# Seven block products for the output projection of layer 0, with operand sums made in DRAM

## The chip, the cores and the metric

The kernel runs on one core of a Trainium2 chip. The metric is the device time of one execution in microseconds, the median of three runs: 1484.73 (1484.15 to 1485.28). A profiled execution, with its trace, gives the rows that are quoted below.

## The reference

Two diffusion blocks work on 768 tokens (512 image tokens and 256 context tokens) of width 1024. Layer 0 mixes tokens by a long convolution (hyena) and by grouped attention with 8 heads, multiplies both with a gate, and projects the 2048 columns together back to 1024; layer 1 is an mLSTM over the same tokens. What the change touches is the projection at the end of layer 0 and what stands around it:

```python
def combine(hy, att, g_hy, g_att):
    return jnp.concatenate([hy * jax.nn.silu(g_hy), att * jax.nn.silu(g_att)], axis=-1) @ w_out

sh_l, sc_l, ga_l = adaln(c, w_mod[layer], b_mod[layer])      # gate rows: the third part, ga
...
x_lat = x_lat + ga_l[:, None] * rms_norm(y_lat, g_post[layer])
```

## The kernel before

All products keep float32 accuracy by parts: each operand is split into a high and a low half (`split`: ScalarE casts the high half, VectorE subtracts to get the low one), and `mm3` issues three matmuls for one product. Weights come through `load_w`: a slice of 1024 x 256 is loaded in two halves of 512 KB on SP's queue into `wr` (three buffers) and split into `wh` and `wl`.

The program consists of regions: `hy` (convolution), `att` (attention), `out0` (the output projection of layer 0 and the next layer's normalised tokens), `l1a` and `l1b` (layer 1) and `out1` (its output projection). `record` collects the instructions of a region, and `play` issues them in the order of a table of numbers, ORDERS, written out for each region; all engines take their instructions in that order. `SLOTS` says which buffer a tile gets. So all instructions have the line of the helper, L998, in the profile, and are told apart by their tiles: `pj` and `pm` are PSUM tiles of products and small products, `hTh` and `hTl` the transposed tokens (8 k-tiles x 768 tokens) as the stationary operand, `yoh` and `yol` the same for the attention's part of layer 0's mix, `yacc` the accumulated output.

The 2048 columns of the mix are sixteen rows of 768 tokens in a DRAM tensor, `y_scratch` (in the code `y0`): 0 to 7 from the convolution, stored in `hy`, and 8 to 15 from the attention's heads, each stored when its head is done in `att`. The attention loop runs over n = 0 to 23 (head n // 3, a third of the queries n % 3): it transposes probabilities (`turned`), computes the next scores, does what `plan[n]` lists, and multiplies by the values. Through GpSimd's queue the convolution's rows are loaded at n = 18 and 19 and split into `hTh`, `hTl`. `plan` 20 to 23 and `rest` hold `stage_a`: a first half of the projection, 256 output columns at a time, for six token tiles (12 tiles of 24 matmuls, 256 wide).

In `out0`, `out_stages` does the other two column groups of the first half in the same way, then the attention's half of the mix with matmuls 512 wide, added to `yacc` by VectorE; when a token tile's second half of the columns is complete, it is squared, weighed by the gate row `gg`, normalised, added to the input, stored, normalised again (`epi0`) and transposed into `hTh`, `hTl` by `h_tile`, from which layer 1 starts. `gate_rows` makes a gate row out of two 1 MB slices of `w_mod` by 32 small matmuls (32x256, `pm` from `cond`), and spreads it over the partitions by one more. Layer 0's gate rows stand in `out0`, layer 1's at the end of `l1b` (`heads`, the last head).

Layer 1's output projection and its gate products `o` and `z` are already computed as seven block products, with the sums of weight blocks made in DRAM by copies on SP and accumulating transfers on GpSimd's queue (`o_sums`, `w_sums`).

Of the kernel before, what the change touches and what calls it, by code (L numbers as in the profile page):

```python
# [2893 lines left out]
```

## Time and profile before

The profile's page holds busy times of the engines, the DMA queues, the chain of work that ended last, and groups of instructions. PE is TensorE's matmul, PEld its weight loads, DVE VectorE, ACT ScalarE, POOL GpSimd, and SP the engine that issues most transfers.

| | |
|---|---|
| median of the runs | 1484.73 us |
| the profiled execution | 1486.4 us, span 1484.6 us |
| out0 begins, l1a begins (PE) | 743.4, 878.8 us |
| last head stored in att (SP) | 732.0 us |
| layer 1's gate rows (PE, end of l1b) | 1378 to 1400 us |
| DMA, whole span | 230.93 MB, mean 156 GB/s |
| transfers of 512 KB for layer 1's sums | o_sums 28 on POOL, 28 on SP; w_sums 16 on POOL, 16 on SP |

PE is busy over the whole span, so the question for every part is whether PE waits there, and for whom. Windows of 20 us answer that: they give each engine's busy time in the stretch, with the clock granted to TensorE and the share of the DMA engines.

### The profile page before, as it was taken

To read this page: it belongs to the slowest core of one execution; us is meant where nothing else is said; L and a number is where in the kernel's file an instruction comes from. 1 tells how busy PE (TensorE), PEld (TensorE's weight loads), DVE (VectorE), ACT (ScalarE), POOL (GpSimd) and SP (SyncE) were. 2 spreads that over 40 slices of the span, in tenths; PEclk is the share of its full clock that TensorE was granted. 3 is DMA by queue.
4 is the path that set the end of the run, shared out by engine and by line. 5 is a ranking of instruction groups with operands and counts; after the bars stand their busy time and mean duration, and the time that the engine had idled before them with its cause. 6 is when DMAs were issued, how large, how long until landed. Compare 5 with 4: busy or idle time off the path is not lost. (4 is left out here: it accounts for less than half of the span.)

```text
span 1484.6 us, 25597 instructions
## 1 busy us (share of the span) xinstructions
PE 1448.9 (98%) x10122; PEld 1320.5 (89%) x10122; DVE 1071.1 (72%) x1971; ACT 778.8 (52%) x1587; POOL 95.2 (6%) x141
## 2 busy tenths in 40 slices
PE   7999999999999999999999989999999999999997
PEld 5888998989998998989997779999999999989776
DVE  6687777887865666668334899666777777778698
ACT  5643443344435444446332567655766666766554
POOL 1100000001000000000000100000000101110000
PEclk9999999999999999999999999999999999999999
DMA  9655556557331121233463343676654647476575
GB/s 380 212 139 151 142 138 165 147 127 185 86 103 43 55 96 47 90 118 104 152 217 98 114 144 129 228 257 211 221 166 114 161 126 166 141 199 179 203 256 215
DMA packets 63687, 230.93 MB, mean 156 GB/s; under 512 B 7707, under 2 KB 9243, under 8 KB 60784
## 3 DMA queue, kind: packets, MB, share of 16 engines
q1 hardware_dynamic: 55000, 198.63, 38.9%
q0 software_dynamic: 7696, 29.50, 11.3%
q8 instruction: 79, 1.29, 0.3%
q10 hardware_dynamic: 872, 1.18, 0.2%
q14 instruction: 40, 0.33, 0.1%
HBM read 207.23 MB, written 68.19 MB: 186 GB/s over the span
## 5 line engine op out<-in xcount | busy, mean ns | idle before, releaser
L998 PE MATMUL pj<-wl,hTh 128*128 128x256 f32 (+2 forms) x1104 | 315.4, 291 | 1.9 <-DVE wl L998 1.9
L998 PE MATMUL pj<-wh,hTh 128*128 128x256 f32 (+2 forms) x1104 | 316.2, 293 | 0.8 <-ACT qjunk L998 0.4
L998 PE MATMUL pj<-wh,hTl 128*128 128x256 f32 (+2 forms) x1104 | 313.8, 291 | 0.0
L998 PE MATMUL pj<-hTh,wh 128*128 128x512 f32 (+1 forms) x832 | 286.7, 347 | 0.1
L998 PE MATMUL pj<-hTl,wh 128*128 128x512 f32 (+1 forms) x832 | 285.5, 344 | 0.6 <-DVE hTl L998 0.6
L998 PE MATMUL pj<-hTh,wl 128*128 128x512 f32 (+1 forms) x832 | 285.2, 345 | 0.0
L998 DVE TENSOR_TENSOR wl<-wr,wh 128x1024 fp32r<-128x1024 f32 (+1 forms) x154 | 187.6, 1222 | 48.5 <-ACT wh L998 45.7
L998 PEld LDWEIGHTS pj<-wl,hTh 128*128 128x128 f32 x1104 | 206.9, 189 | 7.4 <-DVE wl L998 2.9
L998 PEld LDWEIGHTS pj<-wh,hTh 128*128 128x128 f32 x1104 | 205.9, 188 | 7.4 <-issue 2.0
L998 PEld LDWEIGHTS pj<-wh,hTl 128*128 128x128 f32 x1104 | 206.0, 188 | 4.3 <-issue 1.1
L998 ACT CAST wh<-wr 128x1024 fp32r<-128x1024 f32 (+1 forms) x154 | 159.0, 1044 | 95.5 <-PE pj L998 61.7
L998 PEld LDWEIGHTS pj<-hTh,wh 128*128 128x128 f32 x832 | 156.6, 189 | 19.2 <-DVE vl L998 0.9
L998 PEld LDWEIGHTS pj<-hTh,wl 128*128 128x128 f32 x832 | 156.3, 188 | 18.2 <-DVE wl L998 0.2
L998 PEld LDWEIGHTS pj<-hTl,wh 128*128 128x128 f32 x832 | 156.7, 189 | 17.4 <-DVE hTl L998 0.9
L998 DVE TENSOR_TENSOR PTl<-pj,PTh 128x384 fp32r<-128x384 f32 (+1 forms) x80 | 41.1, 525 | 18.8 <-ACT PTh L998 18.3
L998 ACT CAST PTh<-pj 128x384 fp32r<-128x384 f32 (+1 forms) x80 | 35.5, 458 | 30.6 <-PE pj L998 30.0
L998 DVE TENSOR_TENSOR wl<-ch,wh 128x1024 fp32r<-128x1024 f32 x28 | 34.2, 1221 | 24.1 <-ACT wh L998 24.0
L998 DVE TENSOR_REDUCE mx<-s 128x1 f32<-128x768 f32 (+1 forms) x48 | 37.2, 774 | 11.4 <-PE s L998 11.2
L998 PE MATMUL pm<-Rh,dfa 128*128 128x256 f32 (+1 forms) x192 | 44.9, 305 | 0.0
L998 POOL DMA_DIRECT2D o_sums<-in_o_w_in x28 | 22.8, 814 | 333.9 <-DMA o_sums<-in_o_w_in 167.2
L998 DVE TENSOR_TENSOR med<-big 128x512 f32<-128x512 f32 (+1 forms) x48 | 40.4, 865 | 5.0 <-ACT big L998 4.7
L998 PE MATMUL s<-dfa,qTh 128*128 128x256 f32 (+1 forms) x160 | 42.8, 338 | 0.7 <-ACT hdh L998 0.6
(397 smaller groups left out, 3250.3 us busy)
## 6 DMA issues: line engine op xcount, KB each, us to landing
wr<-in_e_w_in SPq DMA_DIRECT2D x52, 512.0 KB, 5.0
wr<-in_o_w_in SPq DMA_DIRECT2D x50, 512.0 KB, 6.4
o_sums<-in_o_w_in POOLq DMA_DIRECT2D x28, 512.0 KB, 6.7
ch<-o_sums SPq DMA_DIRECT2D x21, 512.0 KB, 4.8
wh<-in_w_mod SPq DMA_DIRECT2D x10, 1024.0 KB, 8.4
wl<-in_w_mod SPq DMA_DIRECT2D x9, 1024.0 KB, 7.6
wr<-in_e_w_out SPq DMA_DIRECT2D x16, 512.0 KB, 4.0
w_sums<-in_o_w_out POOLq DMA_DIRECT2D x16, 512.0 KB, 7.6
```

Of the source, the lines that this page charges most:

```text
L998: x = fn(*a, **k)
```

## The change

Layer 0's output projection becomes seven block products too. The tokens are two halves of 384 (A11, A12 the first half's convolution and attention columns, A21, A22 the second's), the weights four blocks of 1024 x 512 (b11 to b22). Sums of blocks are made in DRAM during `att`: `weight_sums` makes four of weights (`e_sums`), `first_sums` and `head_sums` four of tokens (`y_sums`), the latter as each head is stored. The convolution's rows are stored negated, which makes two of the token sums differences. The first two products (A11 with b11, and S3 = `y_sums` 2 with `e_sums` 2) take the place of `stage_a` in `plan` 20 to 23 and `rest`, 512 columns wide; the other five stand in `out0`, their token forms loaded by `load_form` in four chunks of 384 KB each.

The gate rows of layer 1 (two 1 MB slices each, and 32 small matmuls) are made at the end of `out0`, from where `out0`'s form tiles were; only the spreading stays in `l1b`. `h_tile` transposes into two PSUM tiles, one for what ScalarE reads and one for what VectorE reads. Layer 1 takes the token tiles in the order 0 to 5 in place of 4, 5, 0, 1, 2, 3. The table of orders is new in `att`, `out0`, `l1a`, `l1b` and `out1`, and in a few places in `hy`.

Three places of the new order. GpSimd in `att` (`rq` is a power for a query tile's norm, `cs` and `dfb` receive the convolution's rows), before:

```order
L998 TENSOR_TENSOR rq_4472<-qst_4471,mhalf 128x12
L998 TENSOR_TENSOR rq_4599<-qst_4598,mhalf 128x12
L998 DMA cs_4773<-y_scratch 128x2x768
L998 TENSOR_TENSOR rq_4726<-qst_4725,mhalf 128x12
L998 DMA dfb_4779<-y_scratch 128x2x768
```

and in the changed kernel:

```order
L988 DMA e_sums<-in_e_w_out 128x1024 x2
L988 DMA y_sums<-y_scratch 1024x384
L988 DMA e_sums<-in_e_w_out 128x1024 x5
L988 TENSOR_TENSOR rq_4472<-qst_4471,mhalf 128x12
L988 DMA y_sums<-y_scratch 128x384
L988 DMA e_sums<-in_e_w_out 128x1024
```

The query power rq_4472 now stands behind eight accumulating transfers, and more follow ahead of the third.

SP from the last head's store (`y_scratch<-dec`) on, before (`wh`, `wl` from `w_mod` are raw slices of a gate row, `yraw` a row of the mix):

```order
L998 DMA y_scratch<-dec_4335 128x768
L998 DMA wh_1190_8032<-in_w_mod 128x2048
L998 DMA wl_1191_8033<-in_w_mod 128x2048
L998 DMA wr_8038<-in_e_w_out 128x1024
L998 DMA yraw_8064<-y_scratch 128x768
L998 DMA wr_8039<-in_e_w_out 128x1024
```

and in the changed kernel (`xt` and `yraw` receive chunks of the forms, 7972 to 7975 of F6 and 7991 on of F3):

```order
L988 DMA y_scratch<-dec_4335 128x768
L988 DMA yol_1205_7984<-in_w_mod 128x2048
L988 DMA yoh_1204_7983<-in_w_mod 128x2048
L988 DMA xt_7973<-y_sums 128x2x384
L988 DMA yraw_7972<-y_sums 128x2x384
L988 DMA wr_7979<-e_sums 128x1024
L988 DMA yraw_7974<-y_sums 128x2x384
L988 DMA wr_7978<-e_sums 128x1024
L988 DMA wr_7990<-in_e_w_out 128x1024
L988 DMA xt_7992<-y_sums 128x2x384
L988 DMA xt_7975<-y_sums 128x2x384
```

Eight form chunks of two products are loaded where rows of the mix came one by one, and the chunk with the last head stands behind weights and a chunk of the next product.

TensorE: layer 1's first gate row before, among the last head's products in `l1b`:

```order
L998 MATMUL pm_12039<-Ch_12030,ql_11837 128x258
L998 MATMUL pj_12029<-vh_11834,kal_12012 128x258
L998 MATMUL pm_12015<-wh_2424_12013,cond_67 32x256 x7
L998 MATMUL pm_12015<-wl_2425_12014,cond_67 32x256
L998 MATMUL pj_12048<-wh_2363_11952,hTh 128x256
```

and in the changed kernel, near the end of `out0`, between the last product and the transposes of token tiles:

```order
L988 MATMUL pm_8155<-yoh_1374_8153,cond_67 32x256
L988 MATMUL pj_8067<-wh_1279_8058,hTl 128x512
L988 MATMUL pj_8067<-wh_1279_8058,hTh 128x512
L988 MATMUL pj_8067<-wl_1280_8059,hTh 128x512
L988 MATMUL pm_8151<-yoh_1370_8149,cond_67 32x256
L988 MATMUL pm_8107<-c_ident,xn_8100 128x128 x2
```

The small matmuls of both rows stand one by one between the last product's.

The diff, without the tables and cut to its core:

```diff
@@ h_tile
-            ps = PM((P, 4, P))
+        pair = [PM((P, 4, P)) for _ in range(2)]
...
-                turns[i].append(TE.transpose(ps[:, t, :], xn[hh][:, t * P:(t + 1) * P], ident).ins)
+                turns[i].append(TE.transpose(pair[t // 2][:, 2 * hh + t % 2, :], xn[hh][:, t * P:(t + 1) * P], ident).ins)
...
@@ the convolution's rows
-                V.tensor_tensor(g, g, x0s, ALU.mult)
+                V.scalar_tensor_tensor(g, g, -1.0, x0s, ALU.mult, ALU.mult)
@@ att
+    esum = nc.dram_tensor("e_sums", [4, 2, P, 8, 256], F32).ap()
+    ysum = nc.dram_tensor("y_sums", [4, 8, P, HN], F32).ap()
+    a11, a21 = (y0[0:8, :, n * HN:(n + 1) * HN] for n in range(2))
+    a12, a22 = (y0[8:16, :, n * HN:(n + 1) * HN] for n in range(2))
+
+    def weight_sums(step):
+        t, ((b11, b12), (b21, b22)) = esum, ew_
+        dst, src, add = ((t[0], b12, 0), (t[2], b12, 0), (t[0], b11, 1), (t[2], b22, 1),
+                         (t[1], t[0], 0), (t[1], b22, 1), (t[3], t[1], 0), (t[3], b21, 1))[step]
+        for q in range(2):
+            for k in range(2):
+                sl = slice(4 * k, 4 * k + 4)
+                if add:
+                    G.dma_start(dst[q, :, sl], src[q, :, sl], accum_op=ALU.add)
+                else:
+                    SP.dma_start(dst[q, :, sl], src[q, :, sl])
+
+    def first_sums(step):
+        if step == 0:
+            SP.dma_start(ysum[2], a11)
+            SP.dma_start(ysum[0], a21)
+        elif step == 1:
+            G.dma_start(ysum[2], a21, accum_op=ALU.add)
+        else:
+            SP.dma_start(ysum[1], ysum[2])
+            SP.dma_start(ysum[3], ysum[2])
+
+    def head_sums(h, step):
+        if step == 0:
+            for n in (1, 3, 0):
+                G.dma_start(ysum[n, h], a22[h], accum_op=ALU.add)
+        else:
+            G.dma_start(ysum[3, h], a12[h], accum_op=ALU.add)
...
-    def stage_a(w, cs, i, acc):
-        ps = PJ()[:, :256]
-        last = proj_tok(w, i, ps)
-        S.copy(acc[:, i, cs % 2 * 256:cs % 2 * 256 + 256], ps)
-        return last
+    def first_product(w, n, j):
+        ps = PJ()
+        half_product(ps, wide(w), j, (A11, S3)[n // 2], n % 2, True, True)
...
-    rest = [a1[2], re_, a1[3], ce, a1[4], a1[5]]
+    plan[20] += [ce, u_[0][0], u_[0][1]]
+    plan[21] += [u_[0][2], u_[1][0]]
+    plan[22] += u_[1][1:]
+    plan[23] += u_[2][:2]
+    rest = [u_[2][2]] + u_[3]
...
+        if n % 2 and n < 16:
+            weight_sums(n // 2)
+        if n in (0, 2, 4):
+            first_sums(n // 2)
+        if n > 3:
+            if n % 3 == 1:
+                head_sums(n // 3 - 1, 0)
+            elif n % 3 == 2:
+                head_sums(n // 3 - 1, 1)
@@ out0
-    out_stages(op, ins["e_w_out"], ins["e_w_out2"], part0(0), part0(4), [yacc0, yacc1], ss2,
-               (4, 5, 0, 1, 2, 3), gate_rows(gg, T(op, "xt", (P, D), bufs=2), 0, 2), weigh0, epi0, first=2, w=w_out)
+    head_sums(7, 0)
+    head_sums(7, 1)
...
+    def load_form(tiles, a, src, tag="yraw"):
+        for k in range(0, KT, 2):
+            raw = T(op, tag if k % 4 else "yraw", (P, 2, HN), bufs=2)
+            SP.dma_start(raw, src[k:k + 2].rearrange("t p n -> p t n"))
+            split(*[x[:, k:k + 2, a:a + HN] for x in tiles], raw)
+        return form_of(tiles, a)
...
+    F6 = load_form(hT_, 0, ysum[1], "xt")
+    product0(F6, w_out, 0, q6)
+    row0(0)
+    F3 = load_form(hT_, HN, ysum[3], "xt")
+    product0(F6, wn, 1, q6)
...
+    product0(F3, w, 0, q3)
+    F5 = load_form([T(op, t, (P, KT, HN), F32R) for t in yo[0]], 0, ysum[0])
...
+    A12 = load_form([T(op, t, (P, KT, HN), F32R) for t in yo[1]], 0, a12)
+    product0(F5, wn, 1, q5)
...
+    product0(A12, w, 0, p2)
+    A22 = load_form(hT_, HN, a22)
+    product0(A12, wn, 1, p2)
+    for j in range(3):
+        V.tensor_tensor(c11[:, j], p2[j], c11[:, j], ALU.subtract)
+        weigh0(0, j)
+    for j, q in ((0, 0), (1, 0), (0, 1), (2, 0), (1, 1), (2, 1)):
+        half_product(q4[j], (w, wn)[q], j, A22, q, q == 0, q == 1)
+        if q == 0:
+            epilogue0(j)
+        else:
+            V.tensor_tensor(c21[:, j], q4[j], c21[:, j], ALU.add)
+            weigh0(0, 3 + j)
+            epilogue0(3 + j)
+    rows1 = []
+    for u in range(2):
+        raws = [T(op, t, (P, KT, 256)) for t in yo[u]]
+        for i in range(2):
+            SP.dma_start(raws[i], ins["w_mod"][1, 8 + 2 * u + i])
+        rows1.append(mod_rows(raws).rearrange("p n b -> p (n b)"))
@@ l1b
-            row, spread = gate_rows(gg1, gg1[:, 0], 1, 1)
-            work = [(out_gate, i) for i in range(4)] + [(row, 0)] + [(gate_z, i) for i in range(4)] + [(spread, 0), (row, 1), (spread, 1)]
+            work = [(out_gate, i) for i in range(4)] + [(gate_z, i) for i in range(4)] + [(spread, 0), (spread, 1)]
```

More of the change, by code (lines that the diff above doesn't have):

```diff
@@ L1726, in _body, with wide, form_of, half_product @@
     record("att")
+    def wide(x):
+        return [t.rearrange("p k b -> p (k b)").rearrange("p (k b) -> p k b", b=512) for t in x]
+    def form_of(tiles, a):
+        return lambda k, j: tuple(x[:, k, a + j * P:a + (j + 1) * P] for x in tiles)
+    def half_product(ps, w, j, lhs, q, first, last):
+        for kt in range(4):
+            ins_ = mm3(ps, lhs(4 * q + kt, j), (w[0][:, kt], w[1][:, kt]), first and kt == 0, last and kt == 3)
+        return ins_
+    HN = 384
+    ew_ = [[ins[n][:, hf] for hf in range(2)] for n in ("e_w_out", "e_w_out2")]
+    esum = nc.dram_tensor("e_sums", [4, 2, P, 8, 256], F32).ap()
[28 more added lines that the diff above has]
+            G.dma_start(ysum[3, h], a12[h], accum_op=ALU.add)
     def gate_rows(gg, gp, layer, n):
@@ L1873, in cols @@
             shift(mod_cols(self.r[:, 1]), 1, u)
-    def stage_a(w, cs, i, acc):
-        ps = PJ()[:, :256]
-        last = proj_tok(w, i, ps)
-        S.copy(acc[:, i, cs % 2 * 256:cs % 2 * 256 + 256], ps)
-        return last
-    TILES = (4, 5, 0, 1, 2, 3)
+    hT_ = (hTh, hTl)
+    A11, S3 = form_of(hT_, 0), form_of(hT_, HN)
+    def first_product(w, n, j):
+        ps = PJ()
+        half_product(ps, wide(w), j, (A11, S3)[n // 2], n % 2, True, True)
+        u, v = yacc0[:, j], yacc0[:, 3 + j]
+        if n == 0:
+            S.copy(u, ps)
+        elif n == 1:
+            V.tensor_tensor(u, ps, u, ALU.add)
+        else:
+            V.tensor_tensor(v, ps, u if n == 2 else v, ALU.add)
     Q = [Queries() for _ in range(4)]
@@ L1918, in row_items, with first_items @@
         return using(Slice([ins["w_mod"][1, 4 * part + r.u] for part in (1, 0)], slot, block, True), [r.row])[0], r.cols
-    def a_items(cs, slot, block):
-        return using(Slice(ins["e_w_out"][cs], slot, block), [lambda w, i=i: stage_a(w, cs, i, yacc0) for i in TILES])
+    def first_items(n, slot, block):
+        src = (ew_[0][0], ew_[0][0], esum[2], esum[2])[n][n % 2]
+        return using(Slice(src, slot, block), [lambda w, j=j: first_product(w, n, j) for j in range(3)])
     wq0, wg0, wq1 = Slice(ew[18], 1), Slice(ew[22], 0), Slice(ew[19], 1)
@@ L1946, in _body @@
     rc, cc_ = row_items(1, 17)
-    a0 = a_items(0, 1, 19)
-    a1 = a_items(1, 0, 20)
-    re_, ce = row_items(1, 23)
+    re_, ce = row_items(0, 18)
+    u_ = [first_items(n, 1 - n % 2, (19, 20, 22, 23)[n]) for n in range(4)]
     plan[18] += [rc]
-    plan[19] += [cc_]
-    plan[20] += [a0[0], a0[1]]
-    plan[21] += a0[2:4]
-    plan[22] += a0[4:6]
-    plan[23] += a1[:2]
-    rest = [a1[2], re_, a1[3], ce, a1[4], a1[5]]
+    plan[19] += [cc_, re_]
+    plan[20] += [ce, u_[0][0], u_[0][1]]
[3 more added lines that the diff above has]
+    rest = [u_[2][2]] + u_[3]
     for tag in ("gs", "qTl", "qTh"):
@@ L2065, in _body @@
         it()
-    w_out = load_w(ins["e_w_out"][2])
+    w_out = wide(load_w(esum[1][0]))
     play()
@@ L2179, in _body @@
     op = st.enter_context(pool("out0", side="right"))
-    def load_y0(t, Yh, Yl):
-        raw = T(op, "yraw", (P, NT), bufs=2)
-        SP.dma_start(raw, y0[t])
-        split(Yh, Yl, raw)
     yacc1 = T(op, "yacc", (P, 6, 512))
@@ L2188, in _body @@
     gg = T(op, "gg", (P, 2, D))
-    yoh = T(op, "yoh", (P, KT, NT), F32R)
-    yol = T(op, "yol", (P, KT, NT), F32R)
-    class Part:
-        def __init__(self, k0, load, lhs):
-            self.k0, self.load, self.lhs = k0, load, lhs
-        def __call__(self):
-            self.load()
-    def weigh0(hf, i):
-        y = (yacc0, yacc1)[hf]
-        V.tensor_tensor(y[:, i], y[:, i], gg[:, 0 if i < 4 else 1, hf * 512:(hf + 1) * 512], ALU.mult)
-    def epi0(i, rs):
+    record("out0")
+    c11, c21, c12, c22 = (y[:, n:n + 3] for y in (yacc0, yacc1) for n in (0, 3))
@@ new lines, in _body, with row0, spread0 @@
+    yo = [[f"yo{x}{n}" for x in "hl"] for n in range(2)]
+    head_sums(7, 0)
+    head_sums(7, 1)
+    rows_ = []
+    def row0(u):
+        raws = [T(op, t, (P, KT, 256)) for t in yo[u]]
+        for i in range(2):
+            SP.dma_start(raws[i], ins["w_mod"][0, 8 + 2 * u + i])
+        rows_.append(mod_rows(raws).rearrange("p n b -> p (n b)"))
+        S.dma_start(rows_[u][31:32], ins["b_mod"][0:1, 2048 + 512 * u:2560 + 512 * u])
+    def spread0(u):
+        sl = slice(u * 512, (u + 1) * 512)
+        for c in range(2):
+            ps = PM()
+            TE.matmul(ps, sel[:, c:c + 1].broadcast_to([P, P]), rows_[u], start=True, stop=True)
+            V.tensor_tensor(gg[:, c, sl], ps, gg[:, 1, sl], ALU.mult)
@@ new lines, in load_form, with three, product0 @@
+    def load_form(tiles, a, src, tag="yraw"):
[4 more added lines that the diff above has]
+        return form_of(tiles, a)
+    def three():
+        return [PJ() for _ in range(3)]
+    def product0(lhs, w, q, ps):
+        for j in range(3):
+            half_product(ps[j], w, j, lhs, q, q == 0, q == 1)
@@ new lines, in load0, with y_of @@
+    def load0(src, q):
+        return wide(load_w(src[q]))
+    def y_of(i):
+        return [y[:, i % 3] for y in ((c11, c12) if i < 3 else (c21, c22))]
+    def weigh0(hf, i):
+        y = y_of(i)[hf]
+        g = gg[:, 0 if i < 4 else 1, hf * 512:(hf + 1) * 512]
+        junk = T(op, "junk4", (P, 512), bufs=1)
+        S.activation(junk, y, AF.Square, accum_out=ss2[:, i, hf:hf + 1])
+        if hf and i > 2:
+            V.scalar_tensor_tensor(y, y, -1.0, g, ALU.mult, ALU.mult)
+        else:
+            V.tensor_tensor(y, y, g, ALU.mult)
@@ L2204, in epi0, with epilogue0 @@
+    def epilogue0(i):
+        ss = T(op, "ess", (P, 1), bufs=2)
+        V.tensor_reduce(ss, ss2[:, i], axis=AX.X, op=ALU.add)
+        tmp = T(op, "esst", (P, 1), bufs=2)
+        rs = T(op, "ers", (P, 1), bufs=2)
+        rstd(rs, ss, D, tmp)
         xt = T(op, "xt", (P, D), bufs=2)
         SP.dma_start(xt, ins["x"][i])
-        for hf, y in enumerate((yacc0, yacc1)):
+        for hf, y in enumerate(y_of(i)):
             sl = slice(hf * 512, (hf + 1) * 512)
-            V.scalar_tensor_tensor(xt[:, sl], y[:, i], rs, xt[:, sl], ALU.mult, ALU.add)
+            V.scalar_tensor_tensor(xt[:, sl], y, rs, xt[:, sl], ALU.mult, ALU.add)
@@ L2219, in epi0 @@
             V.tensor_scalar(xn[hf], xt[:, hf * 512:(hf + 1) * 512], rs, None, ALU.mult)
-        return lambda: h_tile(op, i, xn, scl[1], shf[1])
-    def part0(k0):
-        def load():
-            for t in range(4):
-                load_y0(8 + k0 + t, yoh[:, k0 + t], yol[:, k0 + t])
-        return Part(k0, load, lambda kt, i: (yoh[:, k0 + kt, i * P:(i + 1) * P], yol[:, k0 + kt, i * P:(i + 1) * P]))
-    record("out0")
-    out_stages(op, ins["e_w_out"], ins["e_w_out2"], part0(0), part0(4), [yacc0, yacc1], ss2,
-               (4, 5, 0, 1, 2, 3), gate_rows(gg, T(op, "xt", (P, D), bufs=2), 0, 2), weigh0, epi0, first=2, w=w_out)
+        h_tile(op, i, xn, scl[1], shf[1])
@@ new lines, in _body @@
+    S.dma_start(gg[:, 1], ins["g_post"][0:1, :].broadcast_to([P, D]))
+    (b11, b12), (b21, b22) = ew_
+    F6 = load_form(hT_, 0, ysum[1], "xt")
+    wn = load0(esum[1], 1)
+    q6 = three()
+    product0(F6, w_out, 0, q6)
+    row0(0)
+    w = load0(b22, 0)
+    F3 = load_form(hT_, HN, ysum[3], "xt")
+    product0(F6, wn, 1, q6)
+    row0(1)
+    spread0(0)
+    spread0(1)
+    for j in range(3):
+        V.tensor_tensor(c12[:, j], c11[:, j], q6[j], ALU.subtract)
+        V.tensor_tensor(c21[:, j], c21[:, j], q6[j], ALU.subtract)
@@ new lines, in _body @@
+    wn = load0(b22, 1)
+    q3 = three()
+    product0(F3, w, 0, q3)
+    w = load0(esum[0], 0)
+    F5 = load_form([T(op, t, (P, KT, HN), F32R) for t in yo[0]], 0, ysum[0])
+    product0(F3, wn, 1, q3)
+    for j in range(3):
+        V.tensor_tensor(c12[:, j], q3[j], c12[:, j], ALU.add)
+    wn = load0(esum[0], 1)
+    q5 = three()
+    product0(F5, w, 0, q5)
+    w = load0(b21, 0)
+    A12 = load_form([T(op, t, (P, KT, HN), F32R) for t in yo[1]], 0, a12)
+    product0(F5, wn, 1, q5)
+    for j in range(3):
+        V.tensor_tensor(c12[:, j], q5[j], c12[:, j], ALU.add)
+        V.tensor_tensor(c22[:, j], q5[j], c21[:, j], ALU.add)
@@ new lines, in _body @@
+    for j in range(3):
+        weigh0(1, j)
+        weigh0(1, 3 + j)
+    wn = load0(b21, 1)
+    p2 = three()
+    product0(A12, w, 0, p2)
+    w = load0(esum[3], 0)
+    A22 = load_form(hT_, HN, a22)
+    product0(A12, wn, 1, p2)
+    wn = load0(esum[3], 1)
+    for j in range(3):
+        V.tensor_tensor(c11[:, j], p2[j], c11[:, j], ALU.subtract)
+        weigh0(0, j)
+    q4 = three()
+    for j, q in ((0, 0), (1, 0), (0, 1), (2, 0), (1, 1), (2, 1)):
+        half_product(q4[j], (w, wn)[q], j, A22, q, q == 0, q == 1)
+        if q == 0:
+            epilogue0(j)
+        else:
+            V.tensor_tensor(c21[:, j], q4[j], c21[:, j], ALU.add)
+            weigh0(0, 3 + j)
+            epilogue0(3 + j)
@@ L2233, in _body @@
+    rows1 = []
+    for u in range(2):
+        raws = [T(op, t, (P, KT, 256)) for t in yo[u]]
+        for i in range(2):
+            SP.dma_start(raws[i], ins["w_mod"][1, 8 + 2 * u + i])
+        rows1.append(mod_rows(raws).rearrange("p n b -> p (n b)"))
+        S.dma_start(rows1[u][31:32], ins["b_mod"][1:2, 2048 + 512 * u:2560 + 512 * u])
     assert wslot[0] == GSLOT
@@ L2235, in _body @@
     values0 = []
-    for i in (4, 5, 0, 1):
+    for i in range(4):
         values0.append(PJ()[:, :288])
-        last = proj_tok(wv0, i, values0[-1])
-        if i == 4:
-            issue_behind(turns[2], last)
+        proj_tok(wv0, i, values0[-1])
     play()
@@ L2417, in _body @@
     H.wv = wv0
-    for i in (4, 5, 0, 1, 2, 3):
+    for i in range(6):
         H.value(i)
@@ L2699, in _body @@
             k += 1
-    def wide(x):
-        return [t.rearrange("p k b -> p (k b)").rearrange("p (k b) -> p k b", b=512) for t in x]
     def form(tiles, a):
@@ L2710, in part @@
         return ins_
-    hT_ = (hTh, hTl)
     A11, D1 = form(hT_, NL), form(hT_, 0)
```

182 lines of the change are left out of this document (49 added, 133 removed), and 898 rows, old and new, of tables (ORDERS, SLOTS).

## The prediction

> **What bounds the kernel now.** I read the page's first part, then the chain's shares, then windows of 20 us around the place that changes (columns: window, its length, busy us of PE, weight loads, VectorE, ScalarE and POOL with instruction counts, granted clock, DMA share, GB/s).
>
> ```profile
> PE 1448.9 (98%) x10122; PEld 1320.5 (89%) x10122; DVE 1071.1 (72%) x1971; ACT 778.8 (52%) x1587; POOL 95.2 (6%) x141
> PE 31%; DVE 5%; ACT 2%; DMA 2%; issue 1%; POOL 0%; SPq 0%; DVEq 0%; ACTq 0%; POOLq 0%
> 440.00:480.00 40.00, 39.13 (x278) 35.73 (x277) 22.57 (x57) 21.45 (x67) 4.58 (x2) 1.00 0.13 42
> 640.00:680.00 40.00, 39.19 (x270) 35.09 (x269) 28.23 (x68) 19.87 (x50) 4.54 (x4) 1.00 0.32 114
> 740.00:760.00 20.00, 20.00 (x184) 19.18 (x184) 6.96 (x8) 7.90 (x14) 0.00 (x0) 1.00 0.61 224
> 760.00:780.00 20.00, 20.00 (x183) 19.01 (x182) 5.06 (x5) 7.07 (x14) 0.00 (x0) 1.00 0.66 228
> 800.00:820.00 20.00, 20.00 (x83) 15.26 (x82) 11.48 (x16) 7.34 (x13) 0.00 (x0) 1.00 0.11 36
> 840.00:860.00 20.00, 17.58 (x83) 13.60 (x83) 18.07 (x43) 12.83 (x28) 4.35 (x6) 1.00 0.47 177
> 860.00:880.00 20.00, 16.23 (x119) 15.39 (x120) 17.14 (x34) 13.60 (x26) 1.65 (x5) 1.00 0.48 162
> 880.00:900.00 20.00, 20.00 (x122) 17.86 (x120) 18.41 (x29) 13.70 (x21) 0.00 (x0) 1.00 0.31 105
> 900.00:920.00 20.00, 19.32 (x157) 18.88 (x156) 19.65 (x35) 13.52 (x18) 0.00 (x0) 1.00 0.41 132
> 920.00:940.00 20.00, 20.00 (x168) 20.00 (x168) 14.82 (x21) 17.51 (x24) 0.00 (x0) 1.00 0.67 213
> 980.00:1000.00 20.00, 20.00 (x169) 20.00 (x169) 13.41 (x15) 9.71 (x14) 0.00 (x0) 1.00 0.74 253
> 1380.00:1400.00 20.00, 18.86 (x127) 13.98 (x128) 14.14 (x31) 11.48 (x23) 1.03 (x1) 1.00 0.56 186
> 1400.00:1420.00 20.00, 18.43 (x76) 13.71 (x75) 16.82 (x22) 10.56 (x17) 0.00 (x0) 1.00 0.88 314
> 1440.00:1460.00 20.00, 20.00 (x87) 16.13 (x86) 17.24 (x23) 10.94 (x17) 0.00 (x0) 1.00 0.83 286
> ```
>
> PE is the bound: 98% busy, the largest share of the chain, clock 1.00 in every window. But out0 is two stretches. Up to 820 PE is full and VectorE has room (11.48 of 20 us). From 840 to 920 VectorE is full (18.07, 17.14, 18.41, 19.65), and PE has gaps. Two windows price a matmul by its pitch, since busy spans of pipelined matmuls overlap: all 169 of 980 to 1000 are 256 wide, 20/169 = 0.1183 us; those of 1440 to 1460 are 512 wide, 20/87 = 0.2299 us.
>
> The Trainium skill, "Perfetto Trace Analysis", section "Identifying the Most-Contended Engine", says that matmul busy time judges TensorE badly, that weight-load busy time judges it better, and that occupancy is a fair measure for VectorE. The trace agrees at 840 to 860: weight loads 13.60, VectorE 18.07. By that rule columns taken from PE there bring nothing, and the sum below goes the same way.
>
> **1. Columns.** out0's product has 576 matmuls of 256 columns and 288 of 512 now (288 of the narrow ones stand in att): 576 x 0.1183 + 288 x 0.2299 = 134.4 us. Seven products of 3 token tiles x 8 x 3 matmuls are 504 of 512: 115.9 us. PE is relieved of 18.5 us: 1.0 in att (288 narrow ones against 144 wide ones, 34.1 to 33.1), 17.5 in out0. How much of this reaches the end is decided by VectorE's stretch.
>
> **2. out0 up to the first finished quarter.** VectorE's last stretch begins with the first addition of the second half and ends with the last token tile's split:
>
> ```profile
> 743.37 1.11 PE L998 MATMUL pm<-wh,cond 128*32 128x256 f32 x16
> 745.27 0.51 PE L998 MATMUL pj<-wh,hTh 128*128 128x256 f32 x2
> 824.75 0.69 DVE L998 TENSOR_TENSOR yacc<-pj,yacc 128x512 f32<-128x512 f32 x1 [1.10 <-PE pj L998]
> 873.29 1.29 DVE L998 TENSOR_TENSOR hTl<-hf,hTh 128x512 fp32r<-128x512 f32 x2 [0.50 <-ACT hTh L998]
> ```
>
> Now 824.75 - 743.37 = 81.4 us pass before it. After the change the same stretch begins at the first block of A12 times b21. In the new order of PE some 266 matmuls of 512 columns (F6, F3, F5 complete, 50 of A12) and two gate rows stand ahead of it. A row costs at most 745.27 - 743.37 = 1.9 us, half of that if its loads hide; so 266 x 0.2299 + 2 x 0.95 = 63.1 us at full pace. The present stretch holds 4.7 us above its pitch; with that loss it would begin at 67.8 (gain 13.6). I take 8 us of loss, so 71.1 and a gain of **10.4**, because the stretch now also loads 16 form chunks and more weights, and keep 7.0 to 13.6. VectorE has room for it: 16 chunk splits, 15 additions, 6 weighings and 14 weight splits by the rows below are 15.3 + 10.3 + 4.1 + 17.1 = 46.8 of 71 us.
>
> ```profile
> L998 DVE TENSOR_TENSOR yol<-yraw,yoh x8: 948/958/960, 751.4 to 802.8; 128x768 fp32r<-128x768 f32 x8
> L998 DVE TENSOR_TENSOR yacc<-pj,yacc x34: 679/684/693, 788.4 to 1476.3; 128x512 f32<-128x512 f32 x34
> L998 DVE TENSOR_TENSOR yacc<-yacc,gg x20: 680/682/692, 812.7 to 1478.1; 128x512 f32<-128x512 f32 x20
> L998 DVE TENSOR_TENSOR wl<-wr,wh 128x1024 fp32r<-128x1024 f32 (+1 forms) x154 | 187.6, 1222 | 48.5 <-ACT wh L998 45.7
> ```
>
> **3. VectorE's last stretch.** Now 873.29 + 1.29 - 824.75 = 49.8 us, of which its instructions, by the medians of rows as above, need 47.9. In the new order they need 51.8: the splits of A22's last chunk and of one more weight half stand in it, some additions don't. So **+2.0**. It bears two unknowns. The separate PSUM tiles of the transposes take away the mutual waits of this tile, which are
>
> ```profile
>   DVE hf L998: 3.8, 3
>   ACT hf L998: 2.4, 4
> ```
>
> but the stretch is idle for only 1.9 us, so at most -1.9; I take 0, because VectorE is full there. The gate rows of layer 1 (two, 3.8 us of PE) come in below it, where PE has 2.4 and 3.8 us of gaps in the two windows: 0. PE needs 38.9 us in the stretch, less than VectorE. Behind out0 VectorE stays full until 920, so what PE could have gained beyond VectorE isn't carried on; l1a begins 10.4 - 2.0 = **8.4** earlier, between 5.0 and 13.5.
>
> **4. Gate rows out of l1b.** They stand on the chain of waits at the end of l1b (start, us, what):
>
> ```profile
> 1378.06 1.89 PE pm L998 x32
> 1387.01 8.40 DMA wh<-in_w_mod
> 1395.46 1.93 PE pm L998 x14
> 1398.62 1.04 PE pm L998 x16
> 1404.81 5.29 DMA yrab<-y_scratch
> ```
>
> The load of the second row ends the chain there, and its matmuls come late. Gone are 3.8 us of matmuls, and of the gaps of 1380 to 1420 (1.14 + 1.57) an unknown part; the two spread matmuls remain. Bounds 0 and 6.5; behind it a token load of out1 (5.29) is late next, and VectorE's weight splits (16.82 of 20). I take **3.5**.
>
> **5. att.** 1.0 us of columns goes. Added are 16 copies and 16 accumulating transfers of 512 KB for the weights, 4 copies and one accumulation of 1.5 MB and 32 of 192 KB for the tokens: 31 MB in 330 us, 94 GB/s on top of 42 to 114. This is below the 314 at which 1400 to 1420 runs. POOL issues them, at 22.8/28 = 0.8 us each by the rows of layer 1's sums (DMA rows: how many, KB, us to landing):
>
> ```profile
> L998 POOL DMA_DIRECT2D o_sums<-in_o_w_in x28 | 22.8, 814 | 333.9 <-DMA o_sums<-in_o_w_in 167.2
> o_sums<-in_o_w_in POOLq DMA_DIRECT2D x28, 512.0 KB, 6.7
> o_sums<-in_o_w_in SPq DMA_DIRECT2D x14, 512.0 KB, 6.2
> w_sums<-in_o_w_out POOLq DMA_DIRECT2D x16, 512.0 KB, 7.6
> y_scratch<-dec SPq DMA_DIRECT2D x8, 384.0 KB, 7.1
> yraw<-y_scratch SPq DMA_DIRECT2D x8, 384.0 KB, 5.6
> 731.97 0.33 SPq L998 DMA_DIRECT2D y_scratch<-dec  x1
> ```
>
> What queues behind them is POOL's small power for the query norms, and on SP the weights of the next block. I set the added waits against the columns: **0**, bounds -2 and +6. The other orders and the renumbered tokens: 0, bounds +-2.
>
> **Sum.** -8.4 - 3.5 + 0 = -11.9 us. The profiled execution lasted 1486.4 us (span 1484.6), 1.7 above the median of 1484.73; the difference goes onto the median: **1473 us**.
>
> **Rivals.**
> *Full gain.* PE loses no more than now (-13.6), the last stretch gives up its idle 1.9 instead of growing by 2.0 net (-1.9), and l1b gives 6.5: -22, 1463. For it: room on VectorE ahead of the stretch. Against it: 17 to 20 us busy of 20 from 840 on.
> *Loads decide out0.* About 20 MB must land between the last head and the first finished quarter (16 chunks of 384 KB, 18 weight halves of 512 KB, two rows). At the 228 GB/s of 760 to 780 that takes 87 us from 732, so 819 against 824.75: -5.7, +2, l1b -2: 1479. Against it: 286 and 314 in out1.
> *Slower: the last head's sums are exposed.* Its row must be stored (7.1 from 732), accumulated (7.6), loaded (5.6) and split (0.96 on VectorE and, ahead of it, some 0.84 on ScalarE): 22.1 us. Covered are 59 matmuls of half products (13.6), a gate row (1.9) and about 12 us of F6's other heads: 27. Each us above 27 is paid in full; from 27 + 11.9 = 39 on, the gain is gone. If the three transfers take twice their rows, under the loads of the rival before and behind SP's other rows, it is 42.4, and the four heads' accumulations ahead of it on POOL could add 4: 46 - 27 = 19, less 11.9: +7, 1492. Against it: accumulations of more than twice its 192 KB landed in 6.7 and 7.6.
>
> For that rival speaks the Trainium skill, "SBUF — State Buffer", section "Who interferes with whom": a transfer issued by GpSimd can be starved of its descriptors while VectorE holds a shared port. The rows don't show it: 512 KB land in 6.7 us when POOL accumulates and in 6.2 when SP copies, beside a VectorE that is 72% busy. By the rule the sum would be this rival's, by the rows the forecast's; I keep the rows.
>
> *Nothing to see.* The sums' 31 MB cost att its upper bound of 6, l1a's full VectorE takes up part of the rest: -3 to 0, 1483.
>
> **How the numbers follow.** Forecast 0.48 (1467 to 1478), full gain 0.17, loads 0.20, slower 0.08, nothing 0.07. A measurement of this kernel can tell 0.2% (3 us) from no change. Faster by over that: all of the first two, 0.17 of the loads' case, 0.03 of the last: 0.85. Same: 0.03 + 0.04 = 0.07. Slower: 0.08. The range goes from the lower end of the full gain, 1460, to 1483; outside stay the slower case and the edges.
>
> **What would show it.** Right: the windows of out0 hold 87 matmuls per 20 us up to VectorE's last stretch, which begins 67 to 74 us after out0's start and lasts 50 to 53; 1380 to 1400 has no wait for gate rows. Wrong: waits of PE on form chunks or weights in the first 30 us of out0 (the last head, the loads), an att longer by over 2 us with waits for VectorE's query norms or weight splits, or a stretch above 55 us.

## The result, and the profile after

The changed kernel takes 1469.31 us (median, 1468.54 to 1470.08) against 1485.01 of the kernel before in the same measurement: a ratio of 0.9893 (95% interval 0.988 to 0.9906), 15.7 us less. The forecast was 11.9 us less. The sum came near, but two of its terms weren't what they were taken for, and one was a small difference of two larger ones.

The page of the changed kernel, its first line, its queues and its chain by engine:

```profile
PE 1434.9 (98%) x9762; PEld 1293.4 (88%) x9762; DVE 1101.4 (75%) x2007; ACT 793.7 (54%) x1590; POOL 139.1 (9%) x194
q1 hardware_dynamic: 65496, 224.33, 44.3%
q0 software_dynamic: 15968, 45.75, 17.9%
PE 82%; DVE 6%; DMA 6%; ACT 3%; issue 2%; POOL 0%; SPq 0%; POOLq 0%; DVEq 0%; ACTq 0%
```

PE is busy for 14 us less, VectorE for 30 us more, and DMA has 6% of the chain where it had 2%. The places where time was won are read from the start of the same work in both traces, one profiled execution each. In the changed kernel (TensorE's and VectorE's timeline: start, us, engine, operation):

```profile
745.26 1.13 PE L988 MATMUL pm<-yoh,cond 128*32 128x256 f32 x16
815.71 0.69 DVE L988 TENSOR_TENSOR yacc<-pj,yacc 128x512 f32<-128x512 f32 x1
864.09 1.52 DVE L988 TENSOR_TENSOR hTl<-hf,hTh 128x512 fp32r<-128x512 f32 x2
```

| place | before | after | difference |
|---|---|---|---|
| out0 begins on PE | 743.37 | 745.26 | +1.9 |
| VectorE's last stretch in out0 begins | 824.75 | 815.71 | -9.0 |
| it ends | 874.6 | 865.6 | -9.0 |
| layer 1's heads begin (first product with `cvo`) | 1044.3 | 1035.8 | -8.5 |
| last matmul | 1475.9 | 1458.9 | -17.0 |

So out0 begins 2 us later, out0 up to the stretch gained 11, the stretch itself gained nothing, and 8.5 us came behind layer 1's first part. The windows of att and out0 (us busy of PE, weight loads, VectorE, ScalarE, POOL; clock; DMA share; GB/s):

```profile
520.00:540.00 20.00, 17.16 (x111) 15.01 (x110) 10.32 (x24) 7.14 (x16) 4.80 (x4) 1.00 0.81 222
680.00:700.00 20.00, 17.31 (x152) 13.26 (x150) 14.41 (x32) 10.97 (x21) 4.04 (x5) 0.91 0.89 259
740.00:760.00 20.00, 20.00 (x110) 15.40 (x109) 12.26 (x14) 9.92 (x13) 1.65 (x2) 1.00 1.07 359
780.00:800.00 20.00, 20.00 (x83) 15.46 (x83) 12.73 (x15) 9.30 (x11) 0.00 (x0) 1.00 0.81 260
840.00:860.00 20.00, 17.26 (x127) 11.51 (x126) 17.89 (x43) 14.23 (x31) 4.42 (x9) 1.00 0.67 236
```

From 740 to 800 PE is as full as before but for 0.5 us, now beside DMA shares of 0.8 to 1.07. Two windows of att have gaps of PE of 2.8 and 2.7 us where the kernel before has 0 and 0.1. The chain of waits there (start, us, what) names them:

```profile
513.65 12.12 DMA y_scratch<-dec
525.77 0.02 issue
525.79 0.44 DVE dec L988
...
679.31 13.63 DMA wl<-in_w_mod
692.93 0.04 issue
692.98 2.80 PE pj L988 x22
```

The first head's store took 12.1 us to land, and VectorE, which is to write the next head into the same tile, waited for it, and PE for VectorE. The load at 679 took 13.6 us to land. It is the second slice of a row of layer 1's shift and scale, which is made from `w_mod` like a gate row (two expectations below call it one); the new order has moved it forward within att.

**The clock behind a gap.** The clock is 0.91 in the window of 680 to 700. Taken more closely, it is halved for 3.4 us from the end of the second gap on, and without layer 1's rows (experiment 2) for 6.8 us twice:

```profile
692.40:695.80 3.40, 2.82 (x23) 1.12 (x23) 0.89 (x2) 0.00 (x0) 2.22 (x4) 0.50 0.57 152
841.00:847.80 6.80, 4.83 (x16) 3.95 (x17) 4.63 (x13) 3.96 (x10) 1.59 (x2) 0.50 0.56 177
854.70:861.50 6.80, 5.11 (x22) 5.09 (x23) 4.15 (x10) 3.66 (x8) 0.69 (x4) 0.50 0.01 5
```

Every such stretch of these traces begins in a gap of PE or within 2 us after one; not every gap has one (the 2.85 us at 523 in the changed kernel hasn't). Up to the last matmul the profiled executions hold:

| at half clock, us | executions |
|---|---|
| 0 | kernel before, before_no_rows1, before_cut_first, after_no_sums |
| 3.4 | changed kernel, after_row_later |
| 6.8 | after_no_weigh |
| 10.2 | after_cut_A22, after_thin_loads |
| 13.6 | after_cut_F5, after_one_tile |
| 17.0 | after_no_rows1, after_old_l1b, after_old_l1b_no_rows |

Half of such a time is the most that PE can lose by it, so up to 7 us more than in the changed kernel. Where work of PE was taken away and the time stayed, this is a rival of "it cost nothing", and the windows have to decide.

### The profile page after: what moved, and what is told of

Its sections match the earlier page's. It is cut to its first block, busy times and chain, and to the rows that moved or that the text cites. A ratio compares the mean times of both kernels' runs of the same rounds, so it can differ in the third digit from the quotient of the medians.

```text
span 1467.7 us, 25116 instructions
## 1 busy us (share of the span) xinstructions
PE 1434.9 (98%) x9762; PEld 1293.4 (88%) x9762; DVE 1101.4 (75%) x2007; ACT 793.7 (54%) x1590; POOL 139.1 (9%) x194
## 4 chain that ended last, share of the span: by engine, by line
PE 82%; DVE 6%; DMA 6%; ACT 3%; issue 2%; POOL 0%; SPq 0%; POOLq 0%; DVEq 0%; ACTq 0%
PE pj L988 63%; PE pm L988 17%; PE s L988 2%; DVE wl L988 1%; DMA wr<-w_sums 1%; DMA wh<-in_w_mod 1%; DMA wl<-in_w_mod 1%; DMA y_scratch<-dec 1%; DMA wr<-e_sums 1%; ACT wh L988 1%; DVE yacc L988 1%; DMA yraw<-y_sums 1%; DVE xt L988 1%; DVE hh L988 0%; SPq L988 0%
## 5 line engine op out<-in xcount | busy, mean ns | idle before, releaser
L988 PE MATMUL pj<-wh,hTh 128*128 128x256 f32 (+2 forms) x1032 | 310.2, 307 | 2.0 <-ACT hTh L988 1.0
L988 PE MATMUL pj<-wl,hTh 128*128 128x256 f32 (+2 forms) x1032 | 308.8, 304 | 0.0
L988 PE MATMUL pj<-wh,hTl 128*128 128x256 f32 (+2 forms) x1032 | 307.6, 306 | 0.0
L988 DVE TENSOR_TENSOR wl<-wr,wh 128x1024 fp32r<-128x1024 f32 x166 | 201.0, 1217 | 36.4 <-ACT wh L988 35.9
L988 ACT CAST wh<-wr 128x1024 fp32r<-128x1024 f32 x166 | 171.8, 1044 | 84.2 <-PE pj L988 50.5
L988 PEld LDWEIGHTS pj<-wh,hTh 128*128 128x128 f32 x1032 | 193.2, 188 | 13.8 <-ACT hTh L988 1.6
L988 PEld LDWEIGHTS pj<-wl,hTh 128*128 128x128 f32 x1032 | 193.6, 189 | 9.0 <-issue 0.7
L988 PEld LDWEIGHTS pj<-wh,hTl 128*128 128x128 f32 x1032 | 192.4, 188 | 9.9 <-issue 1.5
L988 DVE TENSOR_REDUCE mx<-s 128x1 f32<-128x768 f32 (+1 forms) x48 | 37.0, 772 | 10.4 <-PE s L988 10.3
## 6 DMA issues: line engine op xcount, KB each, us to landing
e_sums<-in_e_w_out POOLq DMA_DIRECT2D x16, 512.0 KB, 10.2
```

Source lines behind the costliest of these rows:

```text
L988: x = fn(*a, **k)
```

## The experiments

Each is given with the ratio to the kernel before, whose median was 1485.56, 1485.96 and 1486.61 in the three sets; where two of them are compared the profiles, one execution of each, have to decide, since the intervals are 3 to 7 us wide.

**1. before_no_rows1: the gate rows' price in l1b.** (A constant copy takes the place of rows.)

```diff
-            rows_[u] = mod_rows(raw_pair([ins["w_mod"][layer, 8 + 2 * u + i] for i in range(2)]))...
+            S.copy(x, vecs[:, :2].unsqueeze(2).broadcast_to([P, 2, 256]))     # layer 1 only
```

> The kernel before, with layer 1's two gate rows left out at the end of l1b (their four 1 MB loads and 32 small matmuls; a constant is copied into the row tiles). Theory 1: the rows cost more there than their 3.8 us of matmuls, because what is queued behind them is late too; then this gains 7 to 9 us, the 8 us that the changed kernel gains from the start of layer 1's heads to the end. Theory 2: the new orders of l1b and out1 bring half of that; then this gains 3.5 to 4.5 us.

Measured 1485.62 us, ratio 1.0002 (0.9993 to 1.0012). Neither theory holds: the rows brought nothing. They stood on the chain that the prediction read, but when they go, other waits grow. From 1370 to 1425 weight loads of PE wait for VectorE's weight splits longer, with the rows and without (waited for: us, times, longest):

```profile
PEld pj L998 <- DVE wl L998: 2.6, 3, 1.9
PEld pj L1000 <- DVE wl L1000: 5.1, 5, 1.8
```

**2. after_no_rows1: the same rows in out0**, left out there in the same way.

> The changed kernel with layer 1's gate rows left out at the end of out0 (same parts left out). Theory 1: VectorE sets the pace of that stretch, and the rows lie below it: 0 to 1 us less. Theory 2: PE sets it: 2 to 3.8 us less.

Measured 1473.94 us, 0.9919 (0.9903 to 0.9935): 4.6 us more by the medians, which neither theory has. The four runs lie between 1470.1 and 1475.9, and the profile is of the fastest; its span is 0.6 us above the changed kernel's. The stretch of VectorE takes 53.5 us there (812.8 to 866.3), not 49.9. PE has gaps of 2.85 us at 840 and 2.4 at 854, which the changed kernel, with the first row's matmuls from 842 on, doesn't have, and the two halvings of the clock shown above, up to 6.8 us lost, stand at them. That the rows filled these gaps and so kept the clock up is suggested by the trace and not tested; shown is that leaving them out gains nothing.

**3 and 4. after_cut_F5 and after_cut_A22: 8.3 us of PE taken away ahead of VectorE's last stretch, and inside it.**

```diff
-    product0(F5, wn, 1, q5)
+    skip(36)                                   # after_cut_F5
...
-        half_product(q4[j], (w, wn)[q], j, A22, q, q == 0, q == 1)
+        skip(12) if q else half_product(q4[j], w, j, A22, 0, True, True)   # after_cut_A22
```

> The changed kernel without the second half of the product F5 (36 matmuls of 512 columns, 8.3 us of PE), which stands ahead of VectorE's last stretch in out0. Theory 1: PE is the bound there: 7 to 8.3 us less. Theory 2: the loads of forms and weights set when that stretch begins: 0 to 3 us less.

> The changed kernel without the second half of the last product of out0, A22 (36 matmuls, 8.3 us of PE as well), which stands inside VectorE's last stretch. Theory 1: VectorE is the bound there: 0 to 2 us less. Theory 2: PE is: 7 to 8.3 us less.

Measured 1469.62 us, 0.9897 (0.9882 to 0.9912), and 1470.91 us, 0.9902 (0.9885 to 0.9918): nothing in both. For A22 that was forecast. For F5 it wasn't: with PE as the bound, as the prediction reads this place, it would be 7 to 8.3 us. Its window shows that PE now stands idle for 4.3 us where it was full; VectorE's stretch begins 814.80 - 747.17 = 67.6 us into out0 in place of 70.5, a gain of 2.8, while out0 itself begins 1.9 us later, with 10.2 us at half clock in att:

```profile
780.00:800.00 20.00, 15.68 (x64) 11.66 (x62) 14.02 (x17) 8.86 (x10) 0.00 (x0) 1.00 0.82 260
814.80 0.69 DVE L990 TENSOR_TENSOR yacc<-pj,yacc 128x512 f32<-128x512 f32 x1
```

PE waits there 5.1 us for VectorE's spreading of the gate row (`gg`), which stands behind a weight split whose load landed at 795.4. With A22 cut, 5.45 us of the 8.3 come back as one wait of PE for VectorE (`xn`, until 841.5), and 6.8 us at half clock follow.

**5 and 6. after_thin_loads and before_cut_first: was it the loads, and was PE the bound before?**

```diff
-            SP.dma_start(raw, src[k:k + 2].rearrange("t p n -> p t n"))
-            split(*[x[:, k:k + 2, a:a + HN] for x in tiles], raw)
+            SP.dma_start(raw[:, 0], src[k + 1])
+            split(*[x[:, k:k + 2, a:a + HN] for x in tiles], raw[:, :1].broadcast_to([P, 2, HN]))
...
-                        proj_tok(w, i, ps)             # before_cut_first, column group 3
+                        for kt in range(4):
+                            mm3(ps, hcols(kt, i * P, (i + 1) * P), (w[0][:, kt, :], w[1][:, kt, :]), kt == 0, kt == 3)
```

> The changed kernel with thinner loads in out0's five products: of each form chunk one of its two rows is loaded (192 KB in place of 384), of each weight half one of four k-tiles (128 KB in place of 512), and split as often as before, so VectorE, ScalarE and PE do the same work; some 10 of 17 MB are left out. Theory 1 (new, from the run in which 36 matmuls of F5 brought nothing): out0 up to VectorE's last stretch is paced by loads and the buffers that they wait for; then the stretch begins 3 to 6 us earlier and the kernel gains 2 to 5 us. Theory 2 (of the prediction): PE paces it; then 0 to 1 us.

> The kernel before without half of k in the fourth column group of the first half of out0's product (72 matmuls of 256 columns, 8.5 us of PE), ahead of VectorE's last stretch there. Theory: before the change PE was the bound there: 7 to 8.5 us less. Rival: loads or VectorE paced it then too: 0 to 3 us less.

With thinner loads 1470.45 us, 0.989 (0.9872 to 0.9908): nothing, though the DMA share of 760 to 800 fell to 0.46 and 0.39. The stretch begins 68.8 us into out0 and PE is full up to it (68.80 of 68.80). So it is not the loads alone either. With them thin PE is the bound at 68.8, and with F5 cut the rest is at 67.6 or less: in the changed kernel, at 70.5, the two stand within some 3 us of each other. In the kernel before they stood further apart: 72 narrow matmuls less, 8.5 us of PE, gave 1479.53 us, 0.9953 (0.9935 to 0.997), 4 to 10 us less where 7 to 8.5 were forecast, and the stretch began 817.69 - 741.53 = 76.2 us into out0 in place of 81.4, so 5.2 of the 8.5 reached it:

```profile
741.53 1.11 PE L1000 MATMUL pm<-wh,cond 128*32 128x256 f32 x16
817.69 0.69 DVE L1000 TENSOR_TENSOR yacc<-pj,yacc 128x512 f32<-128x512 f32 x1 [1.10 <-PE pj L1000]
```

**7 and 8. after_old_l1b and after_old_l1b_no_rows: the order of l1b and out1.** The changed kernel up to the end of l1a, then the tables of orders and buffers of the kernel before for l1b and out1, with the gate rows back there; and the same without the rows.

```diff
-    "l1b": [...], "out1": [...]        # the changed kernel's
+    "l1b": [...], "out1": [...]        # those of the kernel before; the buffers of both regions too
```

> The changed kernel with layer 1's gate rows back in l1b and out of out0, and with the order and buffers of the kernel before in l1b and out1; nothing is left out. Theory 1: the new order of l1b and out1 brought the 8 us that came after layer 1's heads began: 6 to 9 us longer than the changed kernel, 1476 to 1479. Theory 2: they came from how l1a ends, which this kernel keeps: 0 to 2 us longer.

> The same, with the rows' four loads and 32 small matmuls left out of l1b. Theory 1 (as the rows brought nothing when left out of the kernel before): within 1.5 us of the same kernel with the rows. Theory 2: where the rest of l1b is earlier the rows are what is late: 4 us or more less.

Measured 1480.14 us, 0.9962 (0.9949 to 0.9976), and 1478.39 us, 0.9947 (0.9929 to 0.9965). By the medians that is 10 us more than the changed kernel, but the rows are missing from the end of out0 here as in experiment 2, with its half clock. Between layer 1's heads and the last matmul the profiles have 430.2 us (1037.8 to 1468.0) with the old order, 429.8 without the rows, and 423.1 in the changed kernel: 7 us. The rows alone are within 2 us, as in the first experiment. From the end of VectorE's stretch to the end of the last matmul (length, then busy us of PE first, as in the windows above), the kernel before, the same without the rows, the old order in the changed kernel, and the changed kernel:

```profile
874.60:1476.30 601.70, 593.63 (x4242) 549.74 (x4240) 459.35 (x802) 381.97 (x785) 38.17 (x63) 1.00 0.60 183
874.20:1474.90 600.70, 589.53 (x4178) 548.05 (x4176) 458.87 (x802) 382.95 (x785) 37.86 (x63) 1.00 0.59 177
866.60:1468.40 601.80, 595.68 (x4263) 552.51 (x4261) 459.31 (x803) 381.57 (x785) 37.14 (x63) 1.00 0.59 184
865.60:1459.30 593.70, 590.48 (x4199) 551.14 (x4197) 459.73 (x806) 380.98 (x784) 36.46 (x64) 1.00 0.58 180
```

In the old order the rows' 64 matmuls are 4.1 us of PE, and when they go PE's idle time grows from 8.1 to 11.2. The changed kernel has both, 5.2 us less work of PE than the old order and idle time of 3.2 in place of 6.1: 8.1 us. So neither part does it alone as far as was run: the rows without the new order bring 1 us, and the new order with the rows still in l1b was not run. With the rows' 4.1 us added to the changed kernel's 590.5 us of PE, the new order alone could be worth at most about 7 of the 8 (an estimate from these windows).

Part of what the new order does is seen in who kept weight loads of PE waiting around the change from l1b to out1 (waited for: us, times, longest): the kernel before (1340 to 1420), the old order in the changed kernel (1330 to 1415), and the changed kernel (1320 to 1410).

```profile
PEld pj L998 <- DVE wl L998: 2.6, 3, 1.9
```

```profile
PEld pj L318 <- DVE wl L318: 3.9, 4, 1.6
```

```profile
PEld pj L988 <- DVE wl L988: 0.3, 1, 0.3
```

The splits of out1's first weights are there in time. All rows of this view together make 9.0 us with the old order and 4.6 in the changed kernel, which waits 2.1 us for a token form of out1 instead.

**9. after_no_sums: the price of the sums in DRAM.** No copy and no accumulating transfer for weights or tokens; the products load blocks of the inputs in their place.

```diff
-                    G.dma_start(dst[q, :, sl], src[q, :, sl], accum_op=ALU.add)
-                else:
-                    SP.dma_start(dst[q, :, sl], src[q, :, sl])
+                skip()
...
+    esum = [ew_[0][1], ew_[1][1], ew_[1][1], ew_[1][0]]
+    ysum = [a22, a22, a11, a22]
```

> The changed kernel without the sums in DRAM: none of the copies and accumulating transfers of weights and tokens is issued, and the products load blocks of the inputs in their place (as many loads and splits as before). Theory 1: the sums' transfers cost att the 2 us by which out0 starts later than before, and the gate row's load that PE waits for at 690 us is late because of them: att ends 2 to 4 us earlier, the kernel gains 2 to 4 us. Theory 2: that wait is one of the order (the row was put there), and the sums lie beside other work: 0 to 1 us.

Measured 1459.77 us, 0.9823 (0.9808 to 0.9837): 9.5 us less than the changed kernel, more than either theory gave. It is there when out0 begins, at 735.37 in place of 745.26. The same work in all three traces is the last product of `hy` with `dfb`; the first score product isn't, since 21 matmuls of att stand ahead of it in the new order only. From there to out0, the kernel before, the changed kernel and the one without sums:

```profile
425.10:743.40 318.30, 314.33 (x2418) 292.31 (x2419) 201.65 (x480) 147.97 (x383) 14.38 (x9) 1.00 0.27 93
424.90:745.30 320.40, 314.31 (x2274) 284.83 (x2276) 213.44 (x496) 151.75 (x381) 58.49 (x61) 0.99 0.73 197
423.20:735.40 312.20, 312.12 (x2275) 284.39 (x2273) 213.28 (x496) 152.83 (x382) 17.52 (x13) 1.00 0.31 106
```

The sums cost 8.2 us: 6.0 us of idle PE, and 2.2 more of busy PE, of which the half clock can be 1.7. Without them PE has no idle time left. Both windows with gaps are full:

```profile
520.00:540.00 20.00, 20.00 (x132) 17.66 (x131) 13.18 (x29) 9.06 (x19) 2.27 (x1) 1.00 0.08 27
680.00:700.00 20.00, 20.00 (x147) 16.88 (x147) 17.80 (x39) 14.81 (x27) 1.44 (x2) 1.00 0.45 160
735.37 1.13 PE L990 MATMUL pm<-yoh,cond 128*32 128x256 f32 x16
```

**10. after_one_tile: the transposes' PSUM tiles.**

```diff
-                turns[i].append(TE.transpose(pair[t // 2][:, 2 * hh + t % 2, :], ...
-                ps = pair[t // 2][:, 2 * hh + t % 2, :]
+                turns[i].append(TE.transpose(pair[hh][:, t, :], ...
+                ps = pair[hh][:, t, :]
```

> The changed kernel with the transposes of h_tile as in the kernel before: each of the two PSUM tiles is read by both ScalarE and VectorE. Theory 1 (of the prediction): VectorE is full in that stretch, so the mutual waits are inside other work: 0 to 2 us longer. Theory 2: the separate tiles are what keeps the last stretch at 50 us though it has more to do: 3 us or more longer.

Measured 1475.82 us, 0.9919 (0.9897 to 0.9942), 6.5 us more by the medians, though the interval touches the changed kernel's and one of the four runs took 1470.71. The profile shows the place: from the stretch's first addition to its last split 56.6 us pass, not 49.9, with the same work. The two engines now wait for each other (816 to 866), in rows that the changed kernel's view doesn't have:

```profile
ACT hf L988 <- DVE hf L988: 3.8, 4, 1.5
DVE hf L988 <- ACT hf L988: 2.5, 3, 1.4
```

Behind the gaps that come of it 3.4 us run at half clock (863.4 to 866.8), at most 1.7 of the 6.7 us.

**11. after_no_weigh: 4.1 us of VectorE's work taken out of the stretch** (the multiplications of the first column half by the gate row).

> The changed kernel without the six multiplications by the gate row of the first column half (VectorE, 128x512, 0.68 us each, 4.1 us), all in the last stretch of out0. Theory 1: VectorE paces that stretch: 2.5 to 4 us less. Theory 2: the chain of PE, ScalarE and VectorE from one token tile to the next paces it: 0 to 1.5 us less.

Measured 1468.95 us, 0.9888 (0.9873 to 0.9903): nothing. The stretch in the changed kernel, without the weighings, without A22's second half, and with shared PSUM tiles, one window each:

```profile
815.70:865.60 49.90, 45.60 (x263) 32.75 (x262) 45.26 (x100) 33.49 (x69) 9.33 (x15) 1.00 0.63 225
```

```profile
816.40:865.90 49.50, 45.64 (x263) 32.79 (x262) 42.22 (x94) 33.43 (x69) 8.42 (x15) 1.00 0.62 224
```

```profile
816.40:866.00 49.60, 38.56 (x228) 26.62 (x228) 45.32 (x100) 33.46 (x69) 9.29 (x15) 0.93 0.63 227
```

```profile
817.30:873.90 56.60, 48.53 (x269) 34.93 (x268) 45.68 (x100) 33.79 (x69) 9.33 (x15) 0.97 0.56 198
```

VectorE has 3 us less to do at full clock, and the length stays: its sum of work doesn't set it. For PE this is less clear. It has 7 us less to do, but 6.8 us at half clock (the 0.93) can hide up to 3.4 us of gain; the 5.45 us that it waited for VectorE speak against PE as the bound. Only when the engines wait for each other's reads of a shared tile does the stretch grow. What remains is a chain that runs from token tile to token tile through all three; that is argued from these four windows and the waits. In the page's views such a chain looks like VectorE at 91%.

**12. after_row_later: the row of 690 us put later.** The 16 small matmuls and their copy go behind the next 16 matmuls of att's order.

```diff
+_later(ORDERS["att"], 2678, 17, 2715)
```

> The changed kernel, whole, with the 16 small matmuls and the copy of the gate row that PE waits for at 690 us put behind the next 8 rows of att's order on TensorE. Theory 1: PE then works while the row's load lands: 1 to 2.5 us less, 1467 to 1468. Theory 2: the load is later still or another wait takes its place: 0.

Measured 1469.56 us, 0.9888 (0.9874 to 0.9903): the same as without. PE's longest gap there fell from 2.5 to 1.1 us, with another name (waits of weight loads and of PE, 685 to 700):

```profile
PEld pj L997 <- ACT mrow L997: 1.3, 1, 1.3
PEld pj L997 <- DMA wl<-in_w_mod: 0.4, 1, 0.4
PE pj L997 <- ACT mrow L997: 1.1, 1, 1.1
```

The small products that need the row now come too soon after it. No half clock stands behind it any more; in this execution one stands behind the first gap instead, which took 3.7 us in place of 2.85, and out0 begins at 745.2 as before.

## Why the prediction came out right, point by point

**Columns: right.** out0 has 360 matmuls of 512 columns in place of 288 of 512 and 288 of 256, which are the 17.5 us, and before the change PE was the bound ahead of the stretch, for 5.2 of 8.5 us taken away (experiment 6).

**Up to the stretch: right in size, short in its reason.** Forecast 71.1 us, a gain of 10.4; it took 815.71 - 745.26 = 70.5, a gain of 10.9. But "I take 8 us of loss" (7.4 by the same working) stood for something that the runs show: PE's pace and that of the rest (loads, splits and buffers) now lie within 3 us of each other. The rival "loads decide out0" put the stretch at 819 - 743.4 = 75.6 us; with F5 cut, where PE waits for the rest, it begins at 67.6, so its price was 8 us off. Which of loads, splits and buffers sets the 67.6 isn't separated. A further cut of PE would bring at most those 3 us.

**The last stretch: the mechanism failed.** "VectorE is full there", and so 51.8 us of instructions make 51.8 us: it took 49.9 and stayed at that when VectorE had less to do. The two PSUM tiles, which I priced at 0 with a bound of 1.9, are worth 5 to 6.7 in the profiled execution: the bound came from the idle time of the old order, while the wait they remove would have been in the new one. The size is loose: the fastest run with shared tiles is only 1.4 us above the changed kernel's median.

**Gate rows out of l1b: the step that failed.** I gave 3.5 us to the rows because they stood on the chain. Their removal alone gives 0 to 2 (experiments 1 and 8): what PE saves comes back as idle time. The 8 us that were won there need the new order of l1b and out1, which stood under "the other orders: 0, bounds +-2". The two terms together, 3.5 and 0, were mis-sized by 4.5; how the 8 us divide between rows and order stays open. That is the larger part of why the gain was 15.7 and not 11.9.

**att: 0 was the difference of two larger numbers.** It lost 2.1 us, the edge of the prediction's own sign of being wrong, but by waits that it hadn't named, for a store and a row's load. The sums cost 8 to 9.5 us (320.4 against 312.2 in att, 9.5 in the medians). The rest of att's change gave 6.1 back: 312.2 against 318.3 before, 3.9 of idle time of PE and 2.2 of its work, of which 1.0 was forecast as columns. My price of the sums went by GB/s: 94 on top of 42 to 114 is far below 314. But accumulated bytes cost more than plain ones. The queues from 440 to 740, without the sums and with them (packets, MB, share of the 16 engines' time):

```profile
q1 hardware_dynamic: 7684, 29.12, 27.6%
q0 software_dynamic: 896, 3.15, 3.2%
```

```profile
q1 hardware_dynamic: 9383, 38.52, 36.5%
q0 software_dynamic: 8285, 18.64, 35.4%
```

Plain bytes cost 0.95% per MB on SP's queue q1 and 1.0% on POOL's q0; the copies that the sums add on q1 cost 0.95% too; the accumulated bytes on q0 cost 32.2% for 15.49 MB, 2.1% per MB. So it is the accumulating and not the queue. The DMA share, not GB/s, shows how full att was.

**The last head's sums: not exposed.** PE is full from 740 to 760, where that rival had its gap, and has one of 0.5 us at 765, for an addition of VectorE. The cover of 27 us held, beside the highest DMA share of the program's windows (1.07).

**Luck in the total.** The stretch's 2.0 us that didn't come and att's 2.1 us that weren't forecast nearly cancel. The range, 1460 to 1483, left room for a gain of 2 or of 25 us.
